# A gated MLP whose up-projection becomes seven block products per tile pair

## The chip, the cores and the metric

The kernel runs on one core of a Trainium2 chip. The metric is the device time of one execution in microseconds (us). TensorE multiplies, VectorE, ScalarE and GpSimd work on elements, and SyncE (SP) issues most DMAs; each engine takes its instructions in the order in which they were written, and semaphores order the engines against each other.

## The reference

One decoder layer on x (1024 tokens x 1024 channels, float32) has three sub-layers, each `x = LayerNorm(alpha * x + f(x))`: a token mixer, a cross-attention into 256 memory tokens, and a gated MLP. The change concerns the MLP and its entry:

```
u = causal_dwconv(x @ w_up, conv_w, conv_b)     # w_up 1024 x 5632; 3 taps along the tokens
g, val = split(u, 2, axis=-1)                   # 2816 channels each
f(x) = (gelu(g) * val) @ w_down                 # w_down 2816 x 1024
```

## The kernel before

Every float32 product is made of three matmuls: both operands are split into a high part (rounded to fp32r, on ScalarE) and a low part (the remainder, on VectorE), and `mm3` (L151 to L154) adds high x high, high x low and low x high in one PSUM bank. `hi_lo` (L79) makes the two parts of an activation, `stage` (L127) those of a weight tile, after `load` (L111) has brought it from DRAM by SP. An object `Split` holds the transposed activation of a token half (512 tokens) as four tiles of 4 x 512: high and low of channels 0 to 511, high and low of channels 512 to 1023. `mm3` with a 512-wide moving operand is one step of the text below.

The order of work is written out by hand. The main line issues matmuls and calls `tick(us)` after each step; `also` (L52) puts a generator in a list of side tasks, and a side task goes on when the clock that `tick` counts has passed the time that it yielded. So the instructions of a side task stand in each engine's queue between those of the main line, at a place set by these due times, and `drain` issues all that is left.

The part before the MLP is the cross-attention's output projection of the second token half. `last_cols` (L876) makes its last 512 columns token tile by token tile (4 tiles of 128 tokens, 8 steps each) and after each tile issues the residual add (`add_res`, VectorE) and a side task for the LayerNorm of that tile (`norm_steps`, L212): statistics on VectorE, a power on GpSimd, centring on ScalarE, scaling on VectorE, and the add of the bias on GpSimd (L234). `channel_step` (L236) then turns a tile: four transposes on TensorE into one bank, high part on ScalarE, low part on VectorE. That is called a turn here. The first half's turns run during `last_cols`; `iter_channels` issues the second half's 16.65 us of clock after the norm.

In the MLP the 22 pairs of up tiles (128 gate channels, 128 value channels) are made one after another by `up_pair` (L962): for each tile 8 steps on the first token half, x2T[0] in pool act, and 8 on the second, x2T[1] in pool act2, into two banks of one PSUM tile of 1024 tokens. Side tasks read both banks: the first tap with bias on ScalarE (L943), two more taps on VectorE (L946), the gelu on ScalarE (L952), gate times value on GpSimd (L956), and the split of the product (L958, L960). The gated tile stays in SBUF. After pairs 3, 5, ... `down_group` (L1003) multiplies two (at the end four) gated tiles into all 1024 tokens x 1024 channels and adds the result to the residual tiles y_t in SBUF (L1020), which hold the layer's second output x2 and at the end the sum. The w_down tiles are split into pool dwp (the last two into wp). In the last group `last_norm` (L1031) normalises and stores each token tile, and the last one is finished in halves.

## Time and profile before

| | |
|---|---|
| three runs | 1480.51, 1480.80, 1481.07 us; median 1480.8 |
| profiled execution | 1481.81 us, of which 1480.0 us span |
| granted TensorE clock, mean | 0.999 |
| busy: TensorE, VectorE, ScalarE, GpSimd | 1453.2, 863.7, 512.2, 244.5 us |
| DMA, whole span | 112.62 MB, mean 76 GB/s |

The span runs from the first to the last instruction; what lies around it is 1.8 us. TensorE counts as busy while matmuls are in flight, so the spacing of their starts says more than the busy share. Idle time of an engine matters only where TensorE waits for it.

### The profile page before, as it was taken

To read this page: it belongs to the slowest core of one execution; us is meant where nothing else is said; L and a number is where in the kernel's file an instruction comes from. 1 tells how busy PE (TensorE), PEld (TensorE's weight loads), DVE (VectorE), ACT (ScalarE), POOL (GpSimd) and SP (SyncE) were. 2 spreads that over 40 slices of the span, in tenths; PEclk is the share of its full clock that TensorE was granted. 3 is DMA by queue.
4 is the path that set the end of the run, shared out by engine and by line. 5 is a ranking of instruction groups with operands and counts; after the bars stand their busy time and mean duration, and the time that the engine had idled before them with its cause. 6 is when DMAs were issued, how large, how long until landed. Compare 5 with 4: busy or idle time off the path is not lost.

```text
span 1480.0 us, 17800 instructions
## 1 busy us (share of the span) xinstructions
PE 1453.2 (98%) x7089; PEld 1210.6 (82%) x7089; DVE 863.7 (58%) x1399; ACT 512.2 (35%) x835; POOL 244.5 (17%) x249
## 2 busy tenths in 40 slices
PE   9899999899999999999999999999999999999997
PEld 7779888798888978888788888888888888888886
DVE  6587666886666675576654535344454544354367
ACT  6455425564353433343333221212121221213131
POOL 3441013411121120010220100001010100001015
PEclk9999999999999999999999999999999999999999
DMA  7314223124263313221221121111111021101102
GB/s 240 116 49 143 72 59 101 47 70 147 69 242 101 127 58 99 73 72 58 69 60 43 72 72 30 58 41 57 40 46 58 29 71 43 58 29 57 43 29 100
DMA packets 31875, 112.62 MB, mean 76 GB/s; under 512 B 3709, under 2 KB 4117, under 8 KB 31152
## 3 DMA queue, kind: packets, MB, share of 16 engines
q1 hardware_dynamic: 30960, 108.17, 22.7%
q0 software_dynamic: 832, 3.31, 0.7%
q8 instruction: 56, 0.92, 0.3%
q14 instruction: 27, 0.22, 0.0%
HBM read 107.26 MB, written 5.78 MB: 76 GB/s over the span
## 4 chain that ended last, share of the span: by engine, by line
PE 82%; DVE 10%; ACT 3%; issue 2%; DMA 1%; POOL 1%; SPq 0%; POOLq 0%; DVEq 0%; ACTq 0%
PE ps L154 9%; PE ps L152 9%; PE ps L153 9%; PE dps L152 5%; PE dps L154 5%; PE dps L153 5%; DVE cv L421 3%; DVE L L470 1%; DVE wlo L138 1%; PE tps L240 1%; ACT whi L136 1%; DVE L L453 1%; ACT L L461 1%; DMA ud<-us 1%; ACT pr L821 1%
## 5 line engine op out<-in xcount | busy, mean ns | idle before, releaser
L138 DVE TENSOR_TENSOR wlo<-raw,whi 128x1024 fp32r<-128x1024 f32 (+2 forms) x144 | 176.6, 1227 | 167.5 <-ACT whi L136 167.3
L136 ACT CAST whi<-raw 128x1024 fp32r<-128x1024 f32 (+3 forms) x161 | 162.8, 1012 | 83.3 <-PE ps L154 68.3
L956 POOL TENSOR_TENSOR u<-u 128x1024 f32<-128x1024 f32 x21 | 60.3, 2873 | 603.8 <-DVE u L946 587.6
L1020 DVE TENSOR_TENSOR y<-dps,y 128x512 f32<-128x512 f32 (+1 forms) x145 | 97.2, 685 | 62.4 <-PE dps L154 62.4
L152 PE MATMUL ps<-aA,whi 128*128 128x512 f32 x336 | 133.2, 396 | 0.4 <-DVE gat L340 0.4
L154 PE MATMUL ps<-aA,wlo 128*128 128x512 f32 x336 | 131.7, 392 | 1.2 <-POOL wlo L138 1.2
L153 PE MATMUL ps<-aA,whi 128*128 128x512 f32 x336 | 131.0, 390 | 0.0
L152 PE MATMUL dps<-dhi,ag 128*128 128x512 f32 (+1 forms) x322 | 125.2, 389 | 0.0
L154 PE MATMUL dps<-dhi,ag 128*128 128x512 f32 (+1 forms) x322 | 125.0, 388 | 0.0
L153 PE MATMUL dps<-dlo,ag 128*128 128x512 f32 (+1 forms) x322 | 125.0, 388 | 0.0
L152 PE MATMUL ps<-whi,aA 128*128 128x512 f32 (+2 forms) x256 | 91.5, 357 | 0.0
L154 PE MATMUL ps<-whi,aA 128*128 128x512 f32 (+2 forms) x256 | 90.0, 352 | 0.4 <-DVE aA L81 0.4
L153 PE MATMUL ps<-wlo,aA 128*128 128x512 f32 (+2 forms) x256 | 89.5, 350 | 0.0
L152 PE MATMUL ps<-whi,aB 128*128 128x512 f32 x192 | 78.3, 408 | 0.0
L154 PEld LDWEIGHTS ps<-aA,wlo 128*128 128x128 f32 x336 | 63.1, 188 | 15.6 <-POOL wlo L138 2.1
L153 PE MATMUL ps<-wlo,aB 128*128 128x512 f32 x192 | 75.8, 395 | 0.0
L154 PE MATMUL ps<-whi,aB 128*128 128x512 f32 x192 | 75.8, 395 | 0.0
L152 PEld LDWEIGHTS ps<-aA,whi 128*128 128x128 f32 x336 | 63.2, 188 | 11.6 <-ACT swv L80 0.5
L153 PEld LDWEIGHTS ps<-aA,whi 128*128 128x128 f32 x336 | 63.2, 188 | 11.3
L154 PEld LDWEIGHTS dps<-dhi,ag 128*128 128x128 f32 x322 | 60.5, 188 | 12.7
L153 PEld LDWEIGHTS dps<-dlo,ag 128*128 128x128 f32 x322 | 60.5, 188 | 12.7
L152 PEld LDWEIGHTS dps<-dhi,ag 128*128 128x128 f32 x322 | 60.5, 188 | 12.7
(977 smaller groups left out, 3384.9 us busy)
## 6 DMA issues: line engine op xcount, KB each, us to landing
raw<-in_w_up SPq DMA_DIRECT2D x44, 512.0 KB, 3.6
raw<-in_w_cm SPq DMA_DIRECT2D x26, 512.0 KB, 3.7
raw<-in_w_down SPq DMA_DIRECT2D x22, 512.0 KB, 3.7
raw<-in_w_out SPq DMA_DIRECT2D x16, 512.0 KB, 4.2
raw<-in_wq SPq DMA_DIRECT2D x16, 512.0 KB, 3.5
raw<-in_wo SPq DMA_DIRECT2D x16, 512.0 KB, 3.6
raw<-in_w_to SPq DMA_DIRECT2D x8, 512.0 KB, 3.6
y<-in_x SPq DMA_DIRECT2D x8, 512.0 KB, 4.0
```

The costliest lines, as they stand in the source:

```text
L136: nc.scalar.copy(hi[:, c], raw[:, c])
L138: eng.tensor_tensor(lo, in0=raw, in1=hi.bitcast(F32), op=SUB)
L152: nc.tensor.matmul(ps, lhsT=ahi, rhs=bhi, start=start, stop=False)
L153: nc.tensor.matmul(ps, lhsT=ahi, rhs=blo, start=False, stop=False)
L154: nc.tensor.matmul(ps, lhsT=alo, rhs=bhi, start=False, stop=stop)
L240: nc.tensor.transpose(ps[:, k * P:(k + 1) * P], y[:, kk * P:(kk + 1) * P], ident)
L421: nc.vector.scalar_tensor_tensor(cv, in0=xc[:, j:j + 512], scalar=mlc[:, i, j:j + 1], in1=cv, op0=MUL, op1=ADD)
L453: nc.vector.tensor_tensor_reduce(L[:, b, kb * P:256], in0=lv[:, b, :], in1=btab[:, i, kb * P:], scale=-1.0, scalar=nsnk[:, i:i + 1], op0=A ...
L461: nc.scalar.activation(Lv, Lv, AF.Exp, bias=nm[:, b:b + 1], scale=-1.0, accum_out=sums[:, b:b + 1])
L470: nc.vector.tensor_scalar(Lv, Lv, sums[:, b:b + 1], None, MUL)
L956: nc.gpsimd.tensor_tensor(ug, in0=ug, in1=u, op=MUL)
L1020: nc.vector.tensor_tensor(yv, in0=ps[:, w], in1=yv, op=ADD)
```

## The change

Write the two token halves of x2 as A (first) and B (second), each with channel halves 1 and 2, and for a pair of up tiles V for the value weights and G for the gate weights, each with input halves 1 and 2. Eight block products, V and G for A and B, become seven. The moving blocks are A1 and A2 (B11, B21 in the code), B2 (B22), and four differences of blocks: T1 = B1 - A1, T3 = B1 - B2, T2 = B2 - T1 and T4 = A2 - T2. The weights' blocks are V1, V2, G2 and four sums: G1 - V1, that plus G2, G1 + G2, and V2 less the second of these. A product P1 to P7 is 4 steps into one bank. Several products go into the same bank one after the other, and ScalarE or VectorE reads the bank in between, while its accumulation is still open.

The sums of weights are made by VectorE for each pair (`sums_of`), and each block is split by ScalarE (`block_hi`) and VectorE (`block_lo`), two to four products ahead. The differences of x2 are made per token tile in `column_steps`, which replaces `iter_channels`: VectorE differences in place in y_t, each followed by a turn. T2 and T3 lie in a new pool xt. As y_t is overwritten, x2 is stored to DRAM by DMAs of the GpSimd queue, and loaded again by SP in the down-projection (`res_load`). For the first four pairs P1 and P2, which need the first token half alone, are made first, into one bank; their other five products follow. For the other pairs the order is P1, P4 and P3 of the pair before, P2, P6, P5, P7.

`gated_steps` makes the taps and the gelu from SBUF tiles of 1024 tokens, multiplies on VectorE instead of GpSimd, and stores the gated tile to DRAM by the GpSimd queue. The down-projection follows after all pairs, for one token half at a time: four token tiles x two column halves fill the eight banks, and for each of 22 blocks a gated tile's half (256 KB) and a w_down tile (512 KB) are loaded and split (`down_load`, `down_split`). The w_down tile of an even block, and of the first four, goes to pool act, that of an odd one to act2. The last five blocks are made token tile by token tile. The first down products stand ahead of the last pair's P4 and P3. What is left out below is removed code of the functions shown above, helpers, and the tail, which is as before.

```diff
-    def norms(h, ln, us):
+    def norms(h, ln, us, keep=None):
         for tt in range(4):
             yield from norm_steps(y_t[4 * h + tt], ln)
+            if keep is not None:
+                nc.gpsimd.dma_start(keep[4 * h + tt], y_t[4 * h + tt])
             yield us - 1.3 - 0.6
...
+    spill = ctx.enter_context(tc.tile_pool(name="spill", bufs=1, space=bass.MemoryType.DRAM))
...
-    also(norms(0, ln, 8.0), 1.0)
+    x2d = [spill.tile([P, D], F32, name="x2d") for _ in range(8)]
+    also(norms(0, ln, 8.0, x2d), 1.0)
     oT = queries(x1T)
     out_cols(1, "wo", oT, 0, before=settle)
-    x2T = [Split(act, "A"), None]
-    also(channels(y_t[0:4], x2T[0], 1.5))
+    drain()
+    stB.close()
+    xt = ctx.enter_context(tc.tile_pool(name="xt", bufs=2, reuse_waits="tile"))
+    pools["x"] = (wp, xt, "gr", "gr")
...
+    def parts(pool, tag, bufs):
+        return [pool.tile([P, 4, 512], F32R, tag=tag, name="xc", bufs=bufs) for _ in range(2)]
+    x0 = Split(act, "A")
+    B11, B21 = x0.t
+    B22, T1 = parts(act2, "B", 8), parts(act2, "B", 8)
+    T2, T3 = parts(xt, "T", 4), parts(xt, "T", 4)
+    T4 = []
+    also(channels(y_t[0:4], x0, 1.5))
+    def turn(src, dst, tt):
+        ps = mx.tile([P, 512], F32, tag="mx", name="tps")
+        for k in range(4):
+            nc.tensor.transpose(ps[:, k * P:(k + 1) * P], src[:, k * P:(k + 1) * P], ident)
+        c = slice(tt * P, (tt + 1) * P)
+        hi_lo(dst[0][:, :, c], dst[1][:, :, c], ps.rearrange("p (k c) -> p k c", k=4))
+    K1, K2 = slice(0, 512), slice(512, 1024)
+    def sub(dst, x, y):
+        nc.vector.tensor_tensor(dst, in0=x, in1=y, op=SUB)
+    def column_steps(tt):
+        ya, yb = y_t[tt], y_t[4 + tt]
+        yield from norm_steps(yb, ln, 0, 2.15, 2.6)
+        nc.gpsimd.dma_start(x2d[4 + tt], yb)
+        yield 3.4
+        turn(yb[:, K2], B22, tt)
+        yield 1.0
+        sub(ya[:, K1], yb[:, K1], ya[:, K1])
+        yield 0.8
+        turn(ya[:, K1], T1, tt)
+        yield 1.5
+        sub(yb[:, K1], yb[:, K1], yb[:, K2])
+        sub(yb[:, K2], yb[:, K2], ya[:, K1])
+        yield 1.0
+        turn(yb[:, K1], T3, tt)
+        yield 0.8
+        sub(ya[:, K2], ya[:, K2], yb[:, K2])
+        turn(yb[:, K2], T2, tt)
+        turned.append(tt)
...
+                if (tt, j) == (1, 0):
+                    up_loads(-1)
...
-                    tick(0.65)
+                    tick(0.68)
+                if tt == 3 and j:
+                    next(slots)
             add_res(1, tt, 1, pss[tt])
-            if tt == 0:
-                x2T[1] = Split(act2, "B")
-            also(iter_channels(tt, 2.15))
+            also(column_steps(tt))
             tick(0)
-    def iter_channels(tt, us):
-        yield from norm_steps(y_t[4 + tt], ln, 0, us, 2.6)
-        yield 16.65
-        for jj in range(2):
-            channel_step(y_t[4 + tt], x2T[1], tt, jj)
-            yield 0.6
+    NB = 4
+    seq = []
+    for i in range(NB):
+        seq += [("P1", i), ("P2", i)]
+    for i in range(NFT):
+        seq += [("P1" if i >= NB else "P6", i)]
+        if i:
+            seq += [("P4", i - 1), ("P3", i - 1)]
+        seq += [("P2", i), ("P6", i)] if i >= NB else []
+        seq += [("P5", i), ("P7", i)]
+    seq += [("P4", NFT - 1), ("P3", NFT - 1)]
+    where = {s: n for n, s in enumerate(seq)}
+    ad = [spill.tile([P, S], F32, name="ad") for _ in range(NFT)]
...
+    loads = [(where["P1", i] - 4, i, True) for i in range(NB)]
+    for i in range(NFT):
+        n = where["P6" if i < NB else "P1", i] - 4
+        loads += [(n, i, "v"), (n, i, "g")]
...
+    def sums_of(p, i):
+        if p == "P6":
+            s = sums[i] = act2.tile([P, 4, 512], F32, tag="B", name="ws")
+            sub(s[:, 0], graw[i][:, K1], vraw[i][:, K1])
+            nc.vector.tensor_tensor(s[:, 1], in0=graw[i][:, K2], in1=s[:, 0], op=ADD)
+        elif p == "P5":
+            nc.vector.tensor_tensor(sums[i][:, 2], in0=graw[i][:, K1], in1=graw[i][:, K2], op=ADD)
+        elif p == "P3":
+            sub(sums[i][:, 3], vraw[i][:, K2], sums[i][:, 1])
+    def block(p, i):
+        if p in ("P1", "P2"):
+            return vraw[i][:, K1 if p == "P1" else K2]
+        if p == "P4":
+            return graw[i][:, K2]
+        return sums[i][:, {"P7": 0, "P6": 1, "P5": 2, "P3": 3}[p]]
+    def block_hi(p, i):
+        w = wp.tile([P, 2, 512], F32R, tag=("whi", "wlo")[nblk[0] % 2], name="blk")
+        nblk[0] += 1
+        src = block(p, i)
+        nc.scalar.copy(w[:, 0], src)
+        blocks[p, i] = (w, src)
+    def block_lo(p, i):
+        w, src = blocks[p, i]
+        sub(w[:, 1], src, w[:, 0].bitcast(F32))
+    def slot_steps():
+        for n in range(-4, len(seq)):
+            up_loads(n + 5)
+            if n + 4 < len(seq):
+                sums_of(*seq[n + 4])
+            if 0 <= n + 3 < len(seq):
+                block_hi(*seq[n + 3])
+            if 0 <= n + 2 < len(seq):
+                block_lo(*seq[n + 2])
+            yield n
...
-    stP.close()
-    mm = ctx.enter_context(tc.tile_pool(name="mm", bufs=2, space=PSUM))
-    stB.close()
-    tf = ctx.enter_context(tc.tile_pool(name="tf", bufs=2))
-    dwp = ctx.enter_context(tc.tile_pool(name="dwp", bufs=2))
-    pools["d"] = (wp, dwp, "dhi", "dlo")
-    def up_half(w, ps2, h):
-        for k in range(KT):
-            mm3(ps2[:, h, :], w[0][:, k, :], w[1][:, k, :], x2T[h].hi(k), x2T[h].lo(k), k == 0, k == KT - 1)
-            tick(0.65)
...
+    def product(p, i, ps, x, start):
+        w = blocks.pop((p, i))[0]
+        for k in range(4):
+            c = slice(k * P, (k + 1) * P)
+            mm3(ps, w[:, 0, c], w[:, 1, c], x[0][:, k], x[1][:, k], start and k == 0, k == 3, True)
+            tick(0.68)
...
+    def wide():
+        return resp.tile([P, S], F32, tag="res", name="uc")
+    def taps(u, x, i):
+        nc.scalar.activation(u, x, AF.Identity, bias=fconv[:, i, 3:4], scale=fconv[:, i, 2:3])
+        yield 2.0
         for d in (1, 2):
-            nc.vector.scalar_tensor_tensor(u[:, d:S], in0=ps[:, 0:S - d], scalar=fconv[:, i, 2 - d:3 - d],
+            nc.vector.scalar_tensor_tensor(u[:, d:S], in0=x[:, 0:S - d], scalar=fconv[:, i, 2 - d:3 - d],
                                            in1=u[:, d:S], op0=MUL, op1=ADD)
...
-    def value_steps(i, ps2, u, ug, a):
-        yield from conv_steps(i, ps2, u)
-        nc.gpsimd.tensor_tensor(ug, in0=ug, in1=u, op=MUL)
...
+    def gated_steps(i, st):
+        ug = wide()
+        yield from taps(ug, st["c2"], 2 * i)
+        uv = wide()
+        yield 2.7
+        nc.scalar.activation(ug, ug, AF.Gelu_apprx_tanh)
+        yield from taps(uv, st["c1"], 2 * i + 1)
+        yield 2.7
+        nc.vector.tensor_tensor(ug, in0=ug, in1=uv, op=MUL)
+        nc.gpsimd.dma_start(ad[i], ug)
+    def run_slot(p, i):
+        st = pairs.setdefault(i, {})
+        early = i < NB
+        if p == "P1":
+            st["c1"] = wide()
+            st["b"] = bank(mo, "mo")
+            product(p, i, st["b"], B11, True)
+            nc.scalar.copy(st["c1"][:, K2 if early else K1], st["b"])
+        elif p == "P2":
+            ps = st["b"] if early else bank(mo, "mo")
+            product(p, i, ps, B21, not early)
+            if early:
+                nc.scalar.copy(st["c1"][:, K1], ps)
+            else:
+                add(st["c1"][:, K1], ps, st["c1"][:, K1])
+        elif p == "P6":
+            if early:
+                st["b"] = bank(mo, "mo")
+            product(p, i, st["b"], T2, early)
+            if early:
+                add(park[:, i % 2, K1], st["b"], st["c1"][:, K2])
+            else:
+                nc.scalar.copy(st["c1"][:, K2], st["b"])
+        elif p == "P5":
+            st["c"] = bank(mx, "mx")
+            product(p, i, st["c"], T1, True)
+        elif p == "P7":
+            product(p, i, st["b"], T3, False)
+            st["c2"] = wide()
+            if early:
+                add(st["c2"][:, K2], st["b"], st["c1"][:, K2])
+            else:
+                nc.scalar.copy(st["c2"][:, K2], st["b"])
+            add(st["c2"][:, K2], st["c"], st["c2"][:, K2])
+        elif p == "P4":
+            product(p, i, st["b"], T4, False)
+            if early:
+                add(st["c2"][:, K1], st["b"], st["c1"][:, K2])
+            else:
+                nc.scalar.copy(st["c2"][:, K1], st["b"])
+        elif p == "P3":
+            product(p, i, st["c"], B22, False)
+            add(st["c1"][:, K2], st["c"], park[:, i % 2, K1] if early else st["c1"][:, K2])
+            also(gated_steps(i, st), 0.7)
+            del pairs[i]
+    def last_turns():
+        for tt in range(4):
+            while tt not in turned:
+                yield 0.7
+            turn(y_t[tt][:, K2], T4, tt)
+            yield 1.5
+    next(slots)
+    for n, (p, i) in enumerate(seq[:-2]):
+        next(slots)
+        if n == 0:
+            T4 += parts(act2, "B", 8)
+            also(last_turns(), 1.0)
+        if (p, i) == ("P6", 0):
             drain()
+            park = wp.tile([P, 2, D], F32, tag="ln", name="park", bufs=1)
+        run_slot(p, i)
...
+    def down_load(n):
+        while nd[0] <= min(n, len(order) - 1):
+            h, j = order[nd[0]]
+            d = wp.tile([P, 1024], F32, tag="raw", name="raw")
+            nc.sync.dma_start(d, t["w_down"][j])
+            a = xt.tile([P, 512], F32, tag="gr", name="araw")
+            nc.sync.dma_start(a, ad[j][:, 512 * h:512 * h + 512])
+            draw[h, j] = (d, a)
...
+    def down_split(n):
+        while nd[1] <= min(n, len(order) - 1):
+            m = nd[1]
+            down_load(m + 1)
+            d, a = draw.pop(order[m])
+            w = act.tile([P, 2, 1024], F32R, tag="A", name="dw") if m < 4 or m % 2 == 0 else \
+                act2.tile([P, 2, 1024], F32R, tag="B", name="dw")
+            g = wp.tile([P, 2, 512], F32R, tag=("whi", "wlo")[m % 2], name="ag")
+            hi_lo(g[:, 0], g[:, 1], a)
+            hi_lo(w[:, 0], w[:, 1], d)
+            dsp[order[m]] = (g, w)
...
-    acts, downs = [], []
-    for i in range(NFT):
-        acts.append(up_pair(i))
...
-        if i % 2 and 1 < i < NFT - 1:
-            down_group([(acts[j], downs[j]) for j in (i - 3, i - 2)], i == 3, False)
...
+    def res_load(h):
+        for tt in range(4):
+            c = 4 * h + tt
+            y_t[c] = resp.tile([P, D], F32, tag="res", name="y")
+            nc.sync.dma_start(y_t[c], x2d[c])
+    LAST = 5
...
+    def tile_mm(h, j, tts):
+        for tt in tts:
+            if (h, tt, 0) not in banks:
+                open_banks(h, tt)
+            for ch in range(2):
+                down_mm(banks[h, tt, ch], h, j, tt, ch, j == 0, j == NFT - 1)
+    down_split(1)
+    tile_mm(0, 0, (0, 1))
+    ln = load_ln(3)
+    for j, s in enumerate(seq[-2:], 1):
+        next(slots, None)
+        run_slot(*s)
+        down_split(j + 1)
+        tile_mm(0, j, (0, 1))
     drain()
-    down_group([(acts[j], downs[j]) for j in range(NFT - 4, NFT)], False, True)
+    for j in range(3):
+        tile_mm(0, j, (2, 3))
+    res_load(0)
+    for h in range(2):
+        for j in range(0 if h else 3, NFT - LAST):
+            down_split(22 * h + j + 1)
+            if h and j == 4:
+                res_load(1)
+            tile_mm(h, j, range(4))
...
+            for j in range(NFT - LAST, NFT):
+                if tt == 0:
+                    down_split(22 * h + j + 1)
+                for ch in range(2):
+                    if not final:
+                        down_mm(banks[h, tt, ch], h, j, tt, ch, False, j == NFT - 1)
...
+            else:
+                for ch in range(2):
+                    add_res(h, tt, ch, banks[h, tt, ch])
+                also(last_norm(c))
+                tick(0)
```

## Rows read from the trace of the kernel before

**Rows 1.** The page, parts 1 and 2: busy time by engine; granted clock by slice.

```profile
PE 1453.2 (98%) x7089; PEld 1210.6 (82%) x7089; DVE 863.7 (58%) x1399; ACT 512.2 (35%) x835; POOL 244.5 (17%) x249
...
PEclk9999999999999999999999999999999999999999
```

**Rows 2.** The page, part 4: the chain that ended last, by engine.

```profile
PE 82%; DVE 10%; ACT 3%; issue 2%; DMA 1%; POOL 1%; SPq 0%; POOLq 0%; DVEq 0%; ACTq 0%
```

**Rows 3.** Windows: the MLP, first up matmul to last; columns PE PEld DVE ACT POOL.

```profile
739.21:1468.65 729.44, 729.34 (x3188) 595.64 (x3189) 351.14 (x388) 175.19 (x171) 87.22 (x46) 1.00 0.16 51
```

**Rows 4.** Table of waits of TensorE, same stretch: us in total, times, longest.

```profile
PE ups__6974 L152 <- DVE y L646: 0.9, 1, 0.9
```

**Rows 5.** Timeline of TensorE, up-projection: start us, us, operation; 24 matmuls between rows.

```profile
1063.09 0.40 PE L152 MATMUL ups__8884<-aA,whi 128*128 128x512 f32 x1
...
1068.57 0.40 PE L152 MATMUL ups__8884<-aB,whi 128*128 128x512 f32 x1
...
1074.17 0.40 PE L152 MATMUL ups__8951<-aA,whi 128*128 128x512 f32 x1
```

**Rows 6.** Timeline of TensorE: a turn, the MLP's entry, a down group.

```profile
715.62 0.60 PE L240 MATMUL tps<-ident,y 128*128 128x128 f32 x4
...
716.53 0.39 PE L154 MATMUL ps<-whi,aB 128*128 128x512 f32 x1
...
739.21 0.47 PE L152 MATMUL ups__6974<-aA,whi 128*128 128x512 f32 x1 [0.87 <-DVE y L646]
...
765.42 0.40 PE L152 MATMUL ups__7153<-aA,whi 128*128 128x512 f32 x1
...
1098.63 0.39 PE L153 MATMUL dps<-dlo,ag 128*128 128x512 f32 x1
...
1116.31 0.39 PE L153 MATMUL dps<-dlo,ag 128*128 128x512 f32 x1
```

**Rows 7.** Timeline of VectorE and ScalarE, entry of the MLP.

```profile
752.38 3.68 DVE L81 TENSOR_TENSOR aB<-tps,aB 128x512 fp32r<-128x512 f32 x6 [2.50 <-ACT aB L80]
...
761.33 2.60 DVE L946 SCALAR_TENSOR_TENSOR u<-ups__6974,fconv,u 128x1023 f32<-128x1023 f32 x2 [5.26 <-ACT u L943]
...
751.77 3.24 ACT L80 CAST aB<-tps 128x512 fp32r<-128x512 f32 x6 [2.61 <-PE tps L240]
...
760.09 1.21 ACT L943 ACTIVATE u<-ups__6974,fconv 128x1024 f32<-128x1024 f32 x1 [5.08 <-PE ups__6974 L154]
...
765.30 1.06 ACT L952 ACTIVATE u<-u 128x1024 f32<-128x1024 f32 x1
```

**Rows 8.** VectorE: timeline of the last output projection; a group by shape.

```profile
716.88 0.69 DVE L81 TENSOR_TENSOR aA<-tps,aA 128x512 fp32r<-128x512 f32 x1 [0.24 <-ACT aA L80]
...
732.80 0.69 DVE L646 SCALAR_TENSOR_TENSOR y<-y,ps 128x512 f32<-128x512 f32 x1
...
735.04 1.27 DVE L233 SCALAR_TENSOR_TENSOR y<-y,rs,ln 128x1024 f32<-128x1024 f32 x1
...
L960 DVE TENSOR_TENSOR ag<-u,ag 128x1024 fp32r<-128x1024 f32 x21 | 25.7, 1222 | 40.4 <-ACT ag L958 40.4
```

**Rows 9.** Timeline of VectorE and GpSimd, cross-attention of the second half.

```profile
667.31 3.11 DVE L138 TENSOR_TENSOR wlo<-raw,whi 128x1024 fp32r<-128x1024 f32 x1
...
666.93 2.40 POOL L234 TENSOR_TENSOR y<-y,ln 128x1024 f32<-128x1024 f32 x1 [3.07 <-DVE y L233]
```

**Rows 10.** Timeline of GpSimd, the tail.

```profile
1471.60 2.34 POOL L234 TENSOR_TENSOR y<-y,ln 128x1024 f32<-128x1024 f32 x1 [2.51 <-DVE y L233]
```

**Rows 11.** The page, part 6, DMA issues; windows: the first 37 us.

```profile
raw<-in_w_down SPq DMA_DIRECT2D x22, 512.0 KB, 3.7
...
raw<-in_w_ta SPq DMA_DIRECT2D x7, 264.0 KB, 2.7
...
ud<-us POOLq DMA_DIRECT2D x1, 1536.0 KB, 8.2
...
0.00:37.00 37.00, 35.05 (x188) 27.75 (x189) 22.69 (x51) 24.07 (x43) 12.00 (x32) 1.00 0.77 240
```

171 lines of the change are left out of this document (58 added, 113 removed).

## The prediction

> **What bounds the kernel now.** I read the head of the page first: TensorE is busy 98% of a 1480.0 us span, and the clock row shows the upper of its two levels, 2.4 GHz, in every slice [rows 1]. The chain of waits gives TensorE 82% and VectorE 10% [rows 2], and its VectorE pieces lie before the MLP. Then the windows over the part that the diff touches: from 739.21 to 1468.65 us TensorE has 0.1 us without work, while VectorE is busy 48% and ScalarE 24% of it [rows 3]. The table of waits for that part has one TensorE entry, 0.9 us at its start [rows 4]. So here time is the number of matmuls times their spacing, and anything else costs only when it makes TensorE wait.
>
> **Spacing.** One up tile is 24 matmuls on x2T[0] (pool act) and 24 on x2T[1] (pool act2). They take 5.48 and 5.60 us: 0.2283 and 0.2333 each [rows 5]. A pair of tiles takes 4 x 24 = 96 matmuls, 22.16 us. In the down-projection 78 matmuls on a dwp tile take 17.68 us, 0.2267 each [rows 6]. So the pool of the moving operand shows in the spacing.
>
> **The change part by part.** Durations are those of the profiled execution, which took 1481.8 us in all; the median of the three runs is 1.0 us below it, so 1.0 comes off at the end.
>
> *Products.* 7 products of 12 matmuls replace 96 by 84 per pair. P1 and P2 (24) read act tiles, 5.48 us; P3, P4, P5 (36) read act2 tiles, 8.40; P6 and P7 (24) read the new pool xt, 5.48 if it behaves as act, 5.60 if as act2. That is 19.36 to 19.48, I take 19.42: 2.74 saved per pair, 22 x 2.74 = **-60.3** (ends -61.6, -59.0). One product is 2.77 us.
>
> *Entry of the MLP.* That wait (0.87 in the timeline [rows 6]) goes, since P1 of pair 0 takes a bank freed long before. The first 96 up matmuls and 8 turns there took 26.2 us [rows 6] against 22.16 + 8 x 0.45 = 25.8 without waits; together **-1.3**.
>
> *Turns.* One group of four transposes among matmuls: from its start to the second matmul after it 0.91 us, less two spacings of 0.23, so 0.45 us [rows 6]. Before, 16 groups turn x2; now 8 + 20. 12 x 0.45 = **+5.4**.
>
> *Early pairs.* For pairs 0 to 3, P2 goes on in the bank that ScalarE must first copy out after P1, with nothing between, and all later products queue behind it. The nearest row is the 0.87 us wait for a VectorE read of a bank; the 512-wide ScalarE copy is of like length (0.54 spacing [rows 7] against 0.61). 4 x 0.87 = **+3.5** (0 if turns fall between, 4 x 1.2).
>
> *Head.* During the last output projection and the eight early products VectorE must do 38 splits and 21 sums or differences of 128x512 at 0.61 us start to start (six took 3.68 [rows 7]), 36 us; four times the run from a residual add through the statistics to the end of the scale, 3.5 us each [rows 8], 14 us; one weight split 1.2: 51 us. GpSimd's four LayerNorm adds meet this stream: a 1024-wide split that takes 1.22 (as the one in [rows 8]) took 3.11 beside such an add, 1.9 more [rows 9]; 4 x 1.9 = 7.6 brings VectorE to 59. TensorE's own work there is 192 x 0.23 + 28 x 0.45 + 3.5 = 60 us. Both full, each queue in order, and each of four columns now has four turns whose input is a fresh VectorE difference (before, a yield of 16.65 hid that chain). Ends: 0, and 16 turns x 0.9 = 14.4. I take one meeting of 1.9 per column, **+7.6**, as the row is for just that pair of instructions.
>
> The Trainium skill (SBUF — State Buffer, section Who interferes with whom) has a rule that speaks against this head: a VectorE instruction with two SBUF inputs and a GpSimd instruction that reads SBUF shut each other out for the whole instruction. The trace agrees, with the 1.9 us above; by the rule's full length, 2.40 per add, this term would be 9.6 instead of 7.6.
>
> *Pairs 0 to 3, second part.* Five products are 13.85 us. VectorE has per pair 14 instructions of 512 (4 sums, 5 splits, 5 bank adds) at 0.61, two tap pairs at 2.60 [rows 7] and the gate multiply, now its own, 1.2 [rows 8]: 8.6 + 5.2 + 1.2 = 15.0. It falls behind 1.15 per pair, over three such pairs 3.5; the splits are two products ahead, which hides some, but P4 returns to a bank one product after P7 left it. **+3** (ends 0, and 6.5 with 0.69 [rows 8] for each 512, which makes 16.0).
>
> *Pairs 4 to 21.* Again 15.0 on VectorE (7 splits, 3 adds, 4 sums), against 19.42: 77%. ScalarE has 11 of 0.54, two of 1.21 and one of 1.06: 9.4. Each return to an open bank has at least one whole product, 2.77 us, for a copy of 0.54. Laid in order, the tightest split (for P3, behind the second taps) is done half a microsecond early. **+0.5** (ends 0, and 18 x 0.87 = 15.7 if one return per pair waits as at the entry).
>
> *Hand-over.* The first down product stands right behind the last P7. VectorE at that time still has about 1.2 of the second taps, P3's split 0.6, the multiply 1.2, the bank add 0.6, and then the splits of the gated tile 0.6 and the weight 1.2: 5.4, less two matmul spacings that need none of it. **+5.0** (ends 0 and 8, the latter with a tile landing 3 us late). Later steps are covered: 8.3 us of products with the first three tiles stand beside the last pair's 10 us chain, and one more block behind.
>
> *Down-projection.* 1056 matmuls as before. Their moving tile is now in act for even blocks (and the first four) and in act2 for odd ones, mean 0.2300; before, 20 tiles at 0.2267 and the last 2 in wp, taken like act2, gave 0.2273. 1056 x 0.0027 = **+2.9** (ends -0.6, +6.3). Vector work is 1.8 and ScalarE's 1.6 per block of 24 matmuls, 5.5 us. At the change of token half the second block's splits queue behind two residual adds and the statistics, 5.0 of 5.5: **+0.5** (ends 0, 5.5). In the tail GpSimd's add for the tile before the last, which now delays the end [rows 10], starts earlier, as the last tile is 6.9 us instead of 5.3: **-0.4** (0, -2).
>
> *DMAs.* SP: each block loads 512 KB and 256 KB, w_down twice; 768 KB in 5.5 us is 143 GB/s, where the first 37 us moved 240 [rows 11]. x2 comes back as two groups of four 512 KB loads; they stand ahead of block loads in SP, and the splits run some blocks ahead of TensorE. POOL: 8 stores of x2 and 22 of gated tiles; behind a store that waits for the multiply only the next store is queued, and tiles are read 100 us later. A store through DRAM landed in 8.2 us [rows 11]; its buffer is one of eight, of which at most eight are in use at once in the early pairs. Cost 0; if a store held a buffer, VectorE would wait some 3 us per early pair.
>
> Sum: -60.3 - 1.3 + 5.4 + 3.5 + 7.6 + 3 + 0.5 + 5.0 + 2.9 + 0.5 - 0.4 = -33.6. 1481.8 - 33.6 - 1.0 = **1447 us**.
>
> **Rivals.**
> *All waits covered.* Head, pairs, hand-over and half change at 0: 16.6 less, **1431**. For it: the sums lie within one engine's time everywhere but in two short parts. Against: the head's 59 against 60 leaves nothing for order.
>
> *VectorE bounds the seams.* Head 14.4, early pairs 6.5, hand-over 8, and half the late pairs meet one wait (8): +6.8 + 3.5 + 3 + 7.5 = 20.8 more, **1468**. For it: VectorE rises from 48% to some 77% and its queue has no way round a blocked instruction. Against: the splits' lead of two products.
>
> *The other side: open banks.* In a late pair ScalarE's queue holds the gelu (1.06) and the next taps' first step (1.21) in front of the bank copies. The gelu waits for VectorE's taps; if VectorE lags by one tap pair (2.6), the copy after P6 ends 2.6 + 2.3 + 0.5 + 0.3 = 5.7 after it could start, and P7, 2.77 later, waits 2.9. 18 x 2.9 = 52: **1499**. It decides from 33.6 / 18 = 1.9 us per late pair. Against: with due times of 0.68 per three matmuls the copy is put in the queue one product step ahead of the gelu.
>
> *The other side, loads.* If a block's two loads landed one after the other, 3.7 + 2.7 us [rows 11] against 5.5 of products: 44 x 0.9 = 39 more, **1486**. Against: in the first 37 us several were under way at once.
>
> **How the numbers follow.** Forecast 0.56 (its own range 1440 to 1456), covered 0.17, VectorE 0.17, open banks 0.06, loads 0.04. Less than 0.2% (3 us) can't be told from no change here. The first three give faster, 0.90, less 0.01 for a pile-up of all upper ends (about 1480): faster 0.89, same 0.03, slower 0.08. The range reaches to both neighbours, 1431 to 1467.
>
> **What would show it.** In the trace after: 1848 matmuls at P1 to P7 instead of 2112; a late pair of 19.4 us with no TensorE idle time over 0.5; waits of about 0.9 between P1 and P2 of pairs 0 to 3 on ScalarE's copy; some 5 us of idle TensorE before the first down product, ended by a VectorE split; turns in the head waiting for VectorE. Late pairs over 21.3 us, or down blocks over 6.4 us, would make the prediction wrong.

## The result: 21.5 us faster, where 33.6 were predicted

The kernel after the change took 1459.43 us (median of four runs, 1457.32 to 1463.20), the kernel before 1480.93 beside it; ratio 0.9857, 95% interval 0.9837 to 0.9878. The prediction said 1447, range 1431 to 1467: the time lies in that range, but 3.4 us outside the forecast's own 1440 to 1456. So the direction and the main term held, and 12 us of the expected gain were lost. The profiled execution took 1457.32 us; it is the fastest of the four.

In the rows below, aA and xc are the moving blocks of x2 in pool act and in act2 or xt, blk is a weight block, dw and ag are the weight and the gated tile of the down-projection, tps is the bank of a turn, upp that of a product, and uc a tile of the up-projection's results. L147 to L149 are the three matmuls of a step, L900 is VectorE's subtraction, which makes the differences and the low parts of the weight blocks. P1(0) is product P1 of pair 0; a late pair is one of the pairs 4 to 21.

The page of the kernel after, parts 1, 2 and 4, answers to [rows 1] and [rows 2]:

```profile
span 1455.5 us, 18114 instructions
PE 1412.2 (97%) x6876; PEld 1169.0 (80%) x6876; DVE 984.0 (68%) x1614; ACT 627.2 (43%) x1079; POOL 197.9 (14%) x258
...
PE   9999999999999999999978999999999989999997
...
PE 79%; DVE 13%; ACT 4%; issue 2%; POOL 1%; DMA 0%; SPq 0%; DVEq 0%; ACTq 0%; POOLq 0%
```

TensorE was without a gap in the MLP before [rows 3]. Now its row shows two notches there, and VectorE's share of the chain has grown. The windows of the kernel after (PE PEld DVE ACT POOL busy, then the granted clock) answer to [rows 3]. They are cut at the first product, at P6(0), at P1(4), at the end of P7(21) and behind the first down products:

```profile
739.25:788.08 48.83, 33.92 (x161) 25.97 (x160) 35.86 (x53) 19.70 (x35) 7.76 (x6) 0.93 0.26 90
788.08:839.31 51.23, 50.89 (x217) 40.33 (x216) 40.94 (x55) 20.78 (x28) 1.06 (x2) 1.00 0.23 83
839.31:1190.67 351.36, 351.36 (x1513) 283.37 (x1511) 270.81 (x347) 169.12 (x250) 9.56 (x18) 1.00 0.24 82
1190.67:1201.60 10.93, 6.34 (x21) 4.75 (x21) 6.94 (x8) 3.51 (x5) 0.53 (x1) 0.84 0.67 242
1201.60:1440.00 238.40, 238.40 (x1034) 193.51 (x1033) 113.47 (x134) 76.38 (x94) 19.38 (x19) 1.00 0.49 165
```

The third row is the time of 18 late pairs, 19.52 us each, with TensorE never idle: 2.64 less than before, 18 times. Nearly all of TensorE's idle time stands in the first row (15 of 48.8 us, clock 0.93) and the fourth (4.6 of 10.9 us, clock 0.84). The table of TensorE's waits from 700 us on answers to [rows 4], which had one entry:

```profile
PE tps L893 <- DVE y L900: 9.4, 4, 4.8
PE upp L147 <- ACT uc L1069: 2.9, 4, 0.8
PE upp L149 <- DVE blk L900: 2.6, 1, 2.6
PE upp L148 <- DVE dw L81: 2.5, 1, 2.5
PE upp L147 <- ACT dw L80: 2.1, 1, 2.1
PE upp L147 <- DVE y L1222: 1.2, 1, 1.2
PE upp L147 <- DVE uc L1036: 0.3, 1, 0.3
PE tps L893 <- POOL y L229: 0.2, 1, 0.2
```

In this order they are: four turns in the head, waiting for a difference; the bank copies between P1 and P2 of the early pairs; the first product's remainder (the low part of its weight block); the two parts of the first down-projection weights; a bank of the last tile; and two short ones. The longest wait, in the timeline of the kernel after:

```profile
754.57 1.28 DVE L228 SCALAR_TENSOR_TENSOR y<-y,rs,ln 128x1024 f32<-128x1024 f32 x1
755.76 0.69 DVE L900 TENSOR_TENSOR blk<-raw,blk 128x512 fp32r<-128x512 f32 x1
755.99 2.65 POOL L229 TENSOR_TENSOR y<-y,ln 128x1024 f32<-128x1024 f32 x1 [9.08 <-DVE y L228]
756.37 2.83 DVE L900 TENSOR_TENSOR y<-y 128x512 f32<-128x512 f32 x1
...
759.34 1.09 PE L893 MATMUL tps<-ident,y 128*128 128x128 f32 x4 [4.81 <-DVE y L900]
...
763.64 0.63 PE L147 MATMUL upp<-aA,blk 128*128 128x512 f32 x1
...
764.07 0.63 PE L148 MATMUL upp<-aA,blk 128*128 128x512 f32 x1
```

The turn wants the difference of the row at 756.37. That stands on VectorE behind a scale and a block remainder, and then takes 2.83 us instead of 0.69 beside GpSimd's bias addition. After 4.8 us without work TensorE comes back at the lower level, 1.2 GHz (granted 0.50 from 758.5 to 765.2): matmuls stand 0.43 apart. VectorE works without a gap during this wait, and during every other wait of the head that it ends; it is idle at other times, while it waits for ScalarE's copies (1.70 us ahead of 752.24, 2.71 ahead of 768.55).

The hand-over, in TensorE's timeline, and what VectorE had to do first:

```profile
1190.44 0.40 PE L149 MATMUL upp<-xc,blk 128*128 128x512 f32 x1
1192.97 0.50 PE L147 MATMUL upp<-dw,ag 128*128 128x512 f32 x1 [2.14 <-ACT dw L80]
1195.92 0.79 PE L148 MATMUL upp<-dw,ag 128*128 128x512 f32 x1 [2.45 <-DVE dw L81]
...
1199.88 0.40 PE L147 MATMUL upp<-xc,blk 128*128 128x512 f32 x1
```

```profile
1189.19 2.61 DVE L1045 SCALAR_TENSOR_TENSOR uc<-uc,fconv 128x1023 f32<-128x1023 f32 x2 [1.72 <-ACT uc L1042]
1191.71 0.69 DVE L900 TENSOR_TENSOR blk<-ws,blk 128x512 fp32r<-128x512 f32 x1
1192.32 1.22 DVE L1057 TENSOR_TENSOR uc<-uc 128x1024 f32<-128x1024 f32 x1
1193.45 0.68 DVE L1036 TENSOR_TENSOR uc<-upp,uc 128x512 f32<-128x512 f32 x1
1194.05 0.68 DVE L81 TENSOR_TENSOR ag<-araw,ag 128x512 fp32r<-128x512 f32 x1
1194.65 1.22 DVE L81 TENSOR_TENSOR dw<-raw,dw 128x1024 fp32r<-128x1024 f32 x1
```

From the last matmul of P7(21) to the first of P4(21) it is 9.44 us, where 13 spacings would be 3.0. The granted clock is 0.50 from 1195.4 to 1198.7.

### The profile page after: what moved, and what is told of

It is laid out like the page before. It is cut to its first block, busy times and chain, and to the rows that moved or that the text cites. A ratio compares the mean times of both kernels' runs of the same rounds, so it can differ in the third digit from the quotient of the medians.

```text
span 1455.5 us, 18114 instructions
## 1 busy us (share of the span) xinstructions
PE 1412.2 (97%) x6876; PEld 1169.0 (80%) x6876; DVE 984.0 (68%) x1614; ACT 627.2 (43%) x1079; POOL 197.9 (14%) x258
## 3 DMA queue, kind: packets, MB, share of 16 engines
q0 software_dynamic: 5152, 19.04, 3.5%
## 4 chain that ended last, share of the span: by engine, by line
PE 79%; DVE 13%; ACT 4%; issue 2%; POOL 1%; DMA 0%; SPq 0%; DVEq 0%; ACTq 0%; POOLq 0%
PE upp L147 15%; PE upp L149 15%; PE upp L148 15%; PE ps L149 9%; PE ps L147 9%; PE ps L148 9%; DVE cv L418 3%; DVE L L467 1%; DVE wlo L133 1%; PE tps L235 1%; ACT whi L131 1%; DVE y L228 1%; ACT L L458 1%; DVE L L450 1%; ACT pr L819 1%
## 5 line engine op out<-in xcount | busy, mean ns | idle before, releaser
L147 PE MATMUL upp<-xc,blk 128*128 128x512 f32 x440 | 174.1, 396 | 0.3 <-DVE uc L1036 0.3
L149 PE MATMUL upp<-xc,blk 128*128 128x512 f32 x440 | 174.0, 396 | 0.0
L148 PE MATMUL upp<-xc,blk 128*128 128x512 f32 x440 | 173.7, 395 | 0.0
L133 DVE TENSOR_TENSOR wlo<-raw,whi 128x1024 fp32r<-128x1024 f32 (+2 forms) x97 | 119.3, 1230 | 59.8 <-ACT whi L131 59.5
L131 ACT CAST whi<-raw 128x1024 fp32r<-128x1024 f32 (+3 forms) x114 | 114.2, 1001 | 81.2 <-PE ps L149 66.1
L147 PE MATMUL upp<-dw,ag 128*128 128x512 f32 (+1 forms) x357 | 140.2, 393 | 3.4 <-ACT dw L80 2.1
L148 PE MATMUL upp<-dw,ag 128*128 128x512 f32 (+1 forms) x357 | 139.6, 391 | 2.5 <-DVE dw L81 2.5
L149 PE MATMUL upp<-dw,ag 128*128 128x512 f32 (+1 forms) x357 | 139.5, 391 | 0.0
L147 PE MATMUL ps<-aA,whi 128*128 128x512 f32 x336 | 133.5, 397 | 0.3 <-DVE gat L337 0.3
L149 PE MATMUL ps<-aA,wlo 128*128 128x512 f32 x336 | 131.8, 392 | 0.2 <-POOL wlo L133 0.2
L1045 DVE SCALAR_TENSOR_TENSOR uc<-uc,fconv 128x1023 f32<-128x1023 f32 x88 | 112.9, 1283 | 26.6 <-ACT uc L1042 25.0
L149 PEld LDWEIGHTS upp<-xc,blk 128*128 128x128 f32 x440 | 82.5, 187 | 20.8 <-DVE blk L900 0.4
L147 PEld LDWEIGHTS upp<-xc,blk 128*128 128x128 f32 x440 | 82.5, 188 | 20.3 <-issue 0.7
L148 PEld LDWEIGHTS upp<-xc,blk 128*128 128x128 f32 x440 | 82.4, 187 | 19.9
L147 PE MATMUL ps<-whi,aA 128*128 128x512 f32 (+2 forms) x256 | 91.4, 357 | 0.2 <-ACT aA L80 0.2
L81 DVE TENSOR_TENSOR ag<-araw,ag 128x512 fp32r<-128x512 f32 x44 | 31.4, 714 | 89.0 <-ACT ag L80 88.9
L149 PE MATMUL ps<-whi,aA 128*128 128x512 f32 (+2 forms) x256 | 89.9, 351 | 0.2 <-DVE aA L81 0.2
L1036 DVE TENSOR_TENSOR uc<-upp,uc 128x512 f32<-128x512 f32 x66 | 45.5, 689 | 62.9 <-PE upp L149 62.8
L147 PEld LDWEIGHTS upp<-dw,ag 128*128 128x128 f32 x357 | 67.3, 188 | 18.8 <-ACT dw L80 2.6
L148 PEld LDWEIGHTS upp<-dw,ag 128*128 128x128 f32 x357 | 67.4, 189 | 18.2 <-DVE dw L81 3.2
```

The costliest lines, as they stand in the source:

```text
L81: nc.vector.tensor_tensor(lo, in0=src, in1=hi.bitcast(F32), op=SUB)
L131: nc.scalar.copy(hi[:, c], raw[:, c])
L133: eng.tensor_tensor(lo, in0=raw, in1=hi.bitcast(F32), op=SUB)
L147: nc.tensor.matmul(ps, lhsT=ahi, rhs=bhi, start=start, stop=False, skip_group_check=more)
L148: nc.tensor.matmul(ps, lhsT=ahi, rhs=blo, start=False, stop=False, skip_group_check=more)
L149: nc.tensor.matmul(ps, lhsT=alo, rhs=bhi, start=False, stop=stop, skip_group_check=more)
```

## The experiments

Times are medians; each is set against 1459.4 of the kernel after, and each was timed beside the kernel before (1480.4 to 1481.5).

**Is a late pair its matmuls and nothing else?** One product once more, and twice VectorE's remainders:

```
 product(p, i, st["b"], T3, False)          # e7: issued twice for i >= NB
 block_lo(*seq[n + 2])                      # e8: issued twice for late pairs
```

> In the pairs 4 to 21 product P7 is issued twice into its bank (12 more matmuls a pair, nothing more on the other engines; the sums are then wrong). Theory A (a late pair is its matmuls and nothing else, so the eighth product saved is what the change gained): a late pair takes 19.52 + 2.80 = 22.3 us, all of 18 pairs 50.4 us more, the kernel about 1510. Theory B (seams or VectorE hide part of a product): under 2.4 us a pair.

Measured 1506.5 us in one run. A late pair takes 22.32 us (first matmul of P1(4) at 839.18, of P1(10) at 973.09), 2.80 more: theory A, one product more costs 2.80 us to the hundredth. The kernel took 47.1 more, not 50.4; part of the difference lies in the hand-over, where the waits for dw's low part fell from 2.5 to 1.1 us.

> In the pairs 4 to 21 VectorE computes each block's remainder twice, 7 more 128x512 subtractions of 0.69 us (0.61 from start to start) a pair; the result is the same. VectorE is busy 15.0 of a late pair's 19.52 us in the kernel after, so it would be at 19.3 to 19.9. Theory A (VectorE has slack of about 4.5 us a pair, and no wait of TensorE hangs on its order until that is used up): a late pair takes 19.5 to 20.0 us and the kernel 1459 to 1468. Theory B (every pair has seams in which a product waits for a bank that VectorE reads, so that any more work on VectorE shows): 2 us or more a pair, 1495 or more.

Measured 1484.4 in one run; a late pair takes 20.6 us, between the two theories. The window over eight late pairs of this run, and its waits:

```profile
1008.82:1173.77 164.95, 158.16 (x674) 125.42 (x673) 156.95 (x209) 75.27 (x112) 4.25 (x8) 1.00 0.23 77
```

```profile
PE upp L149 <- DVE blk L900: 6.8, 8, 0.9
```

VectorE is busy 156.95 / 8 = 19.6 of 20.6 us, and TensorE waits once per pair, for P3's remainder, the tightest one of the prediction. So most of VectorE's slack was real: 4.6 us more work per pair cost 1.1 us, all of it at that one wait. Whether any smaller addition would cost nothing was not tried.

**The hand-over.** The definitions of `down_load` and `down_split` move up, and the loop gets

```
+        if (p, i) == ("P5", NFT - 1):
+            down_split(0)
         run_slot(p, i)
```

> Only the first splitting of the down-projection's operands (down_split(0), with its loads) is issued ahead of the product P5 of the last pair, instead of after P7. Theory A (the hand-over loses its 6.45 us because the first splits stand behind the last pair's taps, multiply and bank additions on VectorE, and the half clock after it is only the consequence of the two waits of 2.14 and 2.45 us): the gap between the end of P7(21) and the first down product falls under 0.5 us, the following down products stand 0.23 us apart and not 0.42, the second split may still be waited for up to 1 us; the kernel ends 5 to 6.5 us earlier, about 1454. Theory B (VectorE has simply too much to do there, so that the splits moved ahead only push the taps and additions back): the wait moves to P4(21), P3(21) or the second down block, and less than 2.5 us is won.

Measured 1452.7 (ratio 0.9809, 0.9792 to 0.9826), 6.8 us less: theory A. In TensorE's timeline the first down products follow the last P7 at the normal spacing, and neither of the two waits for dw is left:

```profile
1192.61 0.40 PE L149 MATMUL upp<-xc,blk 128*128 128x512 f32 x1
1192.85 0.40 PE L147 MATMUL upp<-dw,ag 128*128 128x512 f32 x1
1193.09 0.39 PE L148 MATMUL upp<-dw,ag 128*128 128x512 f32 x1
```

**The head: lateness, GpSimd, or order?** Three runs. In the first the turns are only due later:

```
-        yield 3.4
+        yield 7.4 if tt else 3.4
         turn(yb[:, K2], B22, tt)
```

> For the last three of the four token columns the turns and differences are issued 4 us of the written clock later, so that products P1 and P2 of the pairs 0 to 3 stand on TensorE ahead of turns whose source VectorE has not made. Theory A (the head lost about 15 us, against 7.6 predicted, because turns were issued before VectorE had their differences, and the half clock followed from the wait of 4.8 us): the waits of turns for VectorE, 9.4 us in all, fall under 3 us, the stretch from P1(0) to P6(0) falls from 48.8 to about 40 to 42 us, and the kernel ends 6 to 9 us earlier. Theory B (VectorE's own chain of normalization, differences and splits takes this long, so that the last column is late whatever stands in front of it): the wait moves to the turns ahead of P6(0) or to that product, the stretch stays over 46 us.

Measured 1457.5 (0.9844, 0.9829 to 0.9858), 1.9 less, and the stretch from P1(0) to P6(0) is 47.6 us: theory B. Neither is clear of the scatter: six other runs have the head of the kernel after unchanged (e1, e4, e5, e7, e8, e14), and in their traces the stretch is 47.5 to 50.3 us. Part of that scatter is the clock, which stands at 0.50 for between 3.4 us (e5) and 10.2 us (e1) of the stretch. The turns of e3 wait 5.4 us instead of 9.4, but the bank copies' waits grow from 2.9 to 4.9. In the code a later turn takes its successors' sources along, since all steps of a column follow one another.

> The four GpSimd additions of the normalization's bias to the second half's tokens are left out (that bias is missing from the result); all else is as in the kernel after. Theory A (GpSimd is a main part of the head's loss: in the kernel after a difference that lay beside such an addition of 2.65 us took 2.83 us on VectorE instead of 0.69, and the normalized tile came 2.65 us later): that difference takes 0.7 us, the waits of turns for VectorE fall from 9.4 to under 4 us, the stretch P1(0) to P6(0) falls from 48.8 to about 40 us, and the kernel ends 6 to 9 us earlier. Theory B (the head is bound by the chain turn, ScalarE copy, VectorE remainder, difference, next turn, that stands in order on VectorE, and GpSimd is only an accident in it): at most the 2.1 us of the stretched difference and what the half clock adds are won, the waits stay over 6 us, the stretch over 45 us.

Measured 1455.5 (0.9836, 0.9819 to 0.9852), 3.9 less; the stretch is 44.3 us, the turns still wait 5.9. No difference takes 2.8 us any more. Neither theory's numbers hold: the stretch is 3 to 6 us below the seven traces with these additions and the old order, so GpSimd is worth some 4 us, about a quarter of the head's 16.6 (table below). The run takes away both the meeting with VectorE and the 2.65 us that a normalised tile waits for its addition; which of the two it was, it can't tell.

In the third run the order of a column is changed:

```
+        sub(ya[:, K1], yb[:, K1], ya[:, K1])
+        sub(yb[:, K1], yb[:, K1], yb[:, K2])
+        yield 1.2
         turn(yb[:, K2], B22, tt)
         yield 1.0
-        sub(ya[:, K1], yb[:, K1], ya[:, K1])
-        yield 0.8
         turn(ya[:, K1], T1, tt)
+        sub(yb[:, K2], yb[:, K2], ya[:, K1])
+        sub(ya[:, K2], ya[:, K2], yb[:, K2])
         yield 1.5
...
```

> In each of the four columns the two differences that need no turn before them are issued first, the other two right after the turn of B22, and the turns follow behind, so that no turn is issued directly behind the difference that makes its source. Counts and sizes are unchanged. Theory A (TensorE waits in the head because each turn's source is queued on VectorE behind remainders that themselves wait for ScalarE's copies of an earlier turn): the waits of turns for VectorE fall from 9.4 to under 4 us, the half clock in the head goes with the wait of 4.8 us, the stretch P1(0) to P6(0) falls to 40 to 43 us, and the kernel ends 5 to 8 us earlier, about 1453. Theory B (VectorE is full in the head, 35.9 us of 48.8 busy and the rest lost to its own waits, whatever the order): the waits move to the block remainders or to P6(0), and less than 2.5 us is won.

Measured 1450.45 (0.9795, 0.9781 to 0.9810), 9.0 less; the stretch is 39.6 us. The waits of this run:

```profile
PE upp L149 <- DVE blk L900: 4.5, 1, 4.5
...
PE tps L893 <- DVE y L900: 1.8, 1, 1.8
```

Theory A, and more than it expected: with the same instructions, 7.6 of the 9.4 us of waits for a difference are gone. The first product's remainder is later (4.5 us instead of 2.6), and the half clock now comes with that wait (0.50 from 743.2 to 749.9). The four runs lie within 1.2 us; those of the kernel after were 5.9 apart.

**Why xt and act2 are slower than act.** The prediction read from [rows 5, 6] that the moving operand's pool shows in the spacing. Two paddings:

```
+    act2.tile([P, 24], F32, name="pad2", bufs=1)      # e4, e5: 96 bytes ahead of act2's tiles
+    const.tile([P, 8], F32, name="pad1")              # e5 alone: 32 bytes ahead of wp and act
```

> Only 96 unused bytes a partition are put at the start of the pool that holds act2's tiles, so that act2 and the pools behind it start 96 bytes past a multiple of 128, as the pools wp and act already do. Nothing else changes. In the kernel after, matmuls whose moving and stationary tiles start at the same remainder stand 0.2295 to 0.2304 us apart (aA with blk or whi, pT with Vt), those with different remainders 0.2333 to 0.2341 (xc with blk, whi with aB). Theory A (the remainders must be equal): xc with blk falls from 0.2333 to 0.230, a late pair from 19.52 to about 19.3 us, a down-projection block on act2 from 5.60 to 5.5, and the kernel ends about 8 us earlier. Theory B (the spacing belongs to the pool, its place in SBUF or its traffic): nothing changes, 1459.

> 32 unused bytes a partition in the pool of constants and 96 in act2's pool, so that wp, act, resp, act2 and xt all start at a multiple of 128 bytes. Nothing else changes. In the kernel before, the down-projection's products, whose moving and stationary tiles both started at a multiple of 128, stood 0.2275 us apart, the least of any group. Theory A (equal remainders help, and a remainder of 0 helps most): all groups of 128x512 matmuls near 0.2275, a late pair 19.1 us, a down-projection block 5.46, and the kernel ends 12 to 17 us earlier, about 1444. Theory A' (only equality counts): as with the 96 bytes alone, about 8 us. Theory B (the pool's place): nothing, 1459.

Measured 1458.5 (0.9849, 0.9834 to 0.9863) and 1457.9 (0.9853, 0.9836 to 0.9869); xc with blk at 0.2332 in both. As stated, A and A' are wrong, and B seemed to hold; but neither padding had made the two starts equal in the sense that counts (e14).

**All repairs together.** Beside the two that had won: the first remainder one step sooner, P1 and P2 of two early pairs interleaved, the last bank whole, and another buffer for half of the gated tiles (the diff's core; one load's due time moves along):

```
-    for i in range(NB):
-        seq += [("P1", i), ("P2", i)]
+    for i in range(0, NB, 2):
+        seq += [("P1", i), ("P1", i + 1), ("P2", i), ("P2", i + 1)]
...
-                if tt == 3 and j:
+                if tt == 3:
...
-                    for b in (0, 1) if ch else (None,):
+                    for b in (None,):
```

> The reordered columns (differences first) and the early first split of the down-projection together, and four small steps: the first block remainder is issued one step sooner; the early products run P1(0), P1(1), P2(0), P2(1) and so on, so that ScalarE's copy of a bank lies beside another pair's product; the last tile's second bank is not split into halves; and in the down-projection the blocks whose weights lie in act2 take their gated tile from a buffer at 187904 bytes or above, not below 54 thousand. Theory A (each loss was found in its own place and they add up): from 1450.4, the split 6 us, P1(0)'s wait for its remainder 2.5 to 4, the copies 2.8, the last bank 0.6 us: about 1438; theory C of the matmuls' spacing (in the kernel after, products whose stationary and moving tiles lie on the same side of an address between 86 and 122 thousand bytes stand 0.2275 to 0.2303 us apart, those across it 0.2333) takes 2.5 us more, with blocks on act2 at 0.2285 to 0.2305 and not 0.2335: about 1435. Theory B (VectorE fills the head, so that what one wait gives back the next one takes): the head from P1(0) to P6(0) stays at 38 us or more and the kernel at 1441 or above.

> As the run before it, but of the two differences ahead of the first turn only the one that writes the first half's tile stays there; the other, which overwrites the second half's tile and so must wait until that tile has been written to DRAM (0.6 and 1.2 us of waits on VectorE in the columns of the kernel with the new order), moves behind the second turn. Theory A (those waits hold up the queue of VectorE in the head): 1 to 3 us less than the run before it. Theory B (TensorE doesn't wait for them): the same within 1 us.

Measured 1423.6 (0.9616, 0.9602 to 0.9630) and 1422.6 (0.9608, 0.9592 to 0.9624). TensorE's waits in the second, from 700 us on, are these and no others:

```profile
PE tps L893 <- DVE y L900: 5.6, 4, 2.9
PE upp L147 <- DVE uc L1035: 0.5, 1, 0.5
PE upp L149 <- DVE blk L900: 0.4, 1, 0.4
PE upp L148 <- DVE dw L81: 0.4, 1, 0.4
```

The repairs hold together, against theory B of the first (head 34.9 and 35.0 us); the second run's own step won 1.0 at most, its theory B. But 1423.6 is 11 to 14 less than the first run's two sums, 1435 and 1438: every product had become faster, 2.72 us on all operands, also in stages that no edit touched. The undivided last bank had made a statistics tile smaller, and with it act2 and all pools behind it had moved down by 32 bytes. That gave a new theory, tried on both kernels with nothing but this line:

```
+    act2.tile([P, 56], F32, name="pad2", bufs=1)      # 224 bytes
```

> The kernel after with 224 unused bytes a partition at the start of act2's pool, and nothing else changed. In the two best versions all products came to stand 0.2267 us apart, also those of stages that were not touched (whi with aB at 430 us: 0.2333 before, 0.2288 there); there a smaller statistics tile had moved act2 and all pools behind it 32 bytes down, from 122368 to 122336. Theory D (two matmul operands that start at the same remainder of 256 bytes are read at full speed; 122336, 53984 and 29408 all leave 224, 122368 leaves 0, the 96-byte pad left 96 against 224, the aligned version 128 against 0, which is why both won nothing): with act2 at 122592, remainder 224, a late pair takes 19.04 us instead of 19.52, a down-projection block 5.44 instead of 5.53, whi with aB 0.229, and the kernel ends 16 to 17 us earlier, about 1443. Theory E (one of the small steps of the best versions did it, the ring of gated tiles or the interleaved products): nothing, 1458 to 1459. Theory C (sides of an address): nothing either, which the untouched blocks of the best versions already speak against.

> The kernel before with the same 224 bytes, nothing else. Its up-projection has one token half in act (0.2267 us) and one in act2 (0.2333), its down-projection is at 0.2275 already. Theory D: a pair goes from 22.16 to about 21.8 us, 22 of them and the queries' products save 8 to 11 us, about 1471; the change is then worth about 28 us between two kernels of equal placement (1471 against 1443) instead of the 21.5 measured. Theory E: 1481.

Measured 1442.1 for the kernel after (0.9734, 0.9720 to 0.9749), 17.3 less, and 1468.55 for the kernel before (0.9915, 0.9898 to 0.9931), 12.9 less where 8 to 11 were expected: theory D, both times, and against C and E. Less these 17.3, the sum of the repairs, 1438, comes to 1420.7, where 1423.6 was measured: they add up but for 3 us. The first matmuls of P1(12) and P1(20), eight late pairs apart, in the kernel after and in the padded one:

```profile
995.47 0.40 PE L147 MATMUL upp<-aA,blk 128*128 128x512 f32 x1
...
1151.63 0.40 PE L147 MATMUL upp<-aA,blk 128*128 128x512 f32 x1
```

```profile
988.51 0.39 PE L147 MATMUL upp<-aA,blk 128*128 128x512 f32 x1
...
1140.84 0.39 PE L147 MATMUL upp<-aA,blk 128*128 128x512 f32 x1
```

156.16 / 8 = 19.52 against 152.33 / 8 = 19.04 us, which is 84 matmuls at 0.2324 and 0.2267. In an untouched stage, eight matmuls apart:

```profile
450.14 0.40 PE L147 MATMUL ps<-whi,aB 128*128 128x512 f32 x1
...
452.00 0.40 PE L149 MATMUL ps<-whi,aB 128*128 128x512 f32 x1
```

```profile
450.23 0.39 PE L148 MATMUL ps<-wlo,aB 128*128 128x512 f32 x1
...
452.04 0.39 PE L147 MATMUL ps<-whi,aB 128*128 128x512 f32 x1
```

0.2325 and 0.2263. Between kernels of equal placement the change is worth 1468.55 - 1442.1 = 26.4 us; the change itself had put more products on operands that disagree (five of seven, against one token half of two).

## Why the prediction was right in direction and 12 us short

The range held because it reached to the neighbouring rivals; the forecast itself was 12 us off. The head was 9.0 us too low. The other terms erred by +2.2 to -2.2 us and cancelled to 0.1, which is luck; the remaining 3.1 us are that the median lies 2.1 above the profiled execution, where the prediction took it 1.0 below. The steps, by the profiled execution, which took 1457.3 where the sum gave 1448.2:

| step | predicted | measured | how it is read |
|---|---|---|---|
| products | -60.3 | -58.1 | 22 x (22.16 - 19.52) |
| early copies | +3.5 | +2.9 | waits on L1069 |
| head | +7.6 | +16.6 | 48.83 - 8 products 22.1 - 16 turns 7.2 - copies 2.9 |
| pairs 0 to 3, second part | +3 | +0.8 | 51.23 - 18 x 2.80 |
| pairs 4 to 21 | +0.5 | 0 | no wait |
| hand-over | +5.0 | +6.4 | 9.44 - 3.0 |
| down-projection, half change | +3.4 | +3.8 | blocks of 5.48 and 5.60; 0.3 |
| tail | -0.4 | 0.0 | wait for L1222 +1.24; last matmul to end 7.37 instead of 8.61 |

These rows come to -27.6, the execution to -24.5. The +3.1 between them is the entry and the turns (+4.1 predicted) together with the part ahead of them: the first turn came 1.6 us earlier than before, through waits in the token mixer that the change doesn't touch, and the first product at the same time (739.25 against 739.21).

*The step that failed is the head.* It priced one meeting of VectorE with GpSimd per column, 1.9 each, and nothing for order, though it says itself that 59 us on VectorE against TensorE's 60 leaves nothing for it. Of the 16.6 us, 9.4 are turns that wait for a difference, 2.6 the first product's remainder and some 2.5 the half clock; an estimated 1.5 of the rest is that the last instruction ahead of each of the nine waits runs out alone (0.40 us for a matmul, where the spacing is 0.23). The mechanism is another: each turn was issued right behind the difference that makes its source, and that difference stood behind remainders that waited for ScalarE's copies of earlier turns. So the engines took turns in waiting: VectorE was busy for 35.9 of the 48.8 us, but in all of the time in which TensorE waited for it. The order alone gave 9.0 us back. GpSimd's part was some 4, and its rule as cited (the Trainium skill, SBUF — State Buffer, section Who interferes with whom) agreed with the trace again: 2.83 us beside an addition of 2.65. The upper end of the term, 14.4, was nearer, and 1459.4 lies nearer to the rival that let VectorE bound the seams (1468) than to the forecast (1447); but that rival's late pairs did not come.

*The clock was no term.* With the wait of 4.81 us in the head, and with the two of 2.14 and 2.45 in the hand-over, the granted clock fell, and the next matmuls ran at 1.2 GHz: 1.3 us more in the hand-over (six gaps of 0.455 instead of 0.233), some 2.5 in the head (nine at 0.43 and two turns). With it the hand-over, whose queue on VectorE was as listed, comes to 6.4 instead of 5.0. The same wait does not always bring it: the 2.63 us ahead of the first product's remainder left the clock at 1.00 in this trace and went with a fall to 0.50 in e4's.

*The products were mis-sized by 2.2 us.* xt was taken half as act, half as act2; it behaves as act2, which is 1.3 of it. The other 0.9 is that aA with blk stood 0.230 apart, where 0.2283 was taken. The prediction took the pool for the cause; e14 and e15, where the pools are the same and only their start moves by 224 bytes, show that it is not.

*The tail came out even.* Two half products of the last tile share one bank now, and the second waited 1.24 us for VectorE's read of the first, for which the prediction had no term. But from the last matmul to the end it is 1.24 us less than before; part of that is the term of -0.4, GpSimd's addition for the tile before, which no longer delays the end.

*Right:* a late pair is its matmuls (e7), VectorE has slack for it (e8), no open bank held up a product of a late pair, and no wait of TensorE there ends with a load. Of the lines said to show it, all came, one in part: 1848 matmuls, 19.5 us a late pair, no idle time there, waits of 0.7 to 0.8 on the copies, and turns waiting for VectorE; of the 4.6 us of waits at the first down products, ScalarE's copy ends the first (2.14) and VectorE's split the second (2.45).

## What to carry to other kernels

Price a chain that crosses three in-order queues by its order, not by each engine's sum: look for every instruction whose source is issued right in front of it, and put its source a step or two earlier. When a step is moved in front of another, list what its first instruction finds ahead of it in each queue, and add something for the slow clock that can come with a wait (here with some waits of 1.9 to 4.8 us). When two uses of one matmul shape differ in spacing, compare where their operands start before blaming the pool. Padding alone won 17.3 us here, nearly as much as the whole change (21.5).

## What the runs showed of the hardware

The spacing of 128x512 matmuls went with the start of both operands' tiles in a partition. The table lists groups of the kernel after, the last two of e4 and e14. Addresses are those of the program's allocation, for the first tile of each pool; what is compared is the remainder of an address after division by 256:

| moving, stationary | starts, remainders by 256 | us |
|---|---|---|
| aA, blk | 53984 and 29408: 224, 224 | 0.230 |
| xc, blk | 130560 and 29408: 0, 224 | 0.233 |
| whi, aB | 29408 and 122368: 224, 0 | 0.232 |
| pT, Vt | 200192 and 130560: 0, 0 | 0.230 |
| e4: xc, blk | 130656 and 29408: 96, 224 | 0.233 |
| e14: xc, blk | 130784 and 29408: 224, 224 | 0.227 |

Equal remainders go with the short spacing, in either pool and on either side; of unequal ones only differences of 32 and 128 bytes were run. That the period is not 512 rests on e12: there xc starts at 130528 and blk at 29408, remainders of 480 and 224 of 512, and they stand 0.227 apart. That it is more than 128 rests on e4 (96 and 224 are equal by 128) and e5 (128 and 0). Why aA with blk also fell, from 0.230 to 0.227 in e14, was not tried; in e4 and e5, where the other pools still disagreed, it was 0.228. The Trainium skill (SBUF — State Buffer, section Who interferes with whom) lists two read ports of TensorE, for the moving operand and for weight loads, and calls them independent; here the two operands' places matter to each other, 0.233 against 0.227 us. How, no run shows.
